# One core, a mixer block with expert lookup: the low half one step later, a pause in the gate build, more rows and loads ahead of stage 2

## The chip, the cores and the metric

One core of one Trainium2 chip runs the whole program. The metric is device time in microseconds: the median of three runs, 3230.48 us before the change.

## What is computed

A block of a language model on 512 tokens of width 2048, in fp32: a mixer (mLSTM and S5 branches), then an expert lookup ("PEER") and a norm. The change lies in the lookup, whose reference is, cut:

```python
s1, i1 = lax.top_k(s[..., 0, :], 16); s2, i2 = lax.top_k(s[..., 1, :], 16)
top_s, pos = lax.top_k(cand_s, 16)            # 8 heads x 16 experts for a token
idx = jnp.take_along_axis(cand_i, pos, axis=-1)
gate = jax.nn.softmax(top_s, axis=-1)
ue = jnp.take(u_tab, it, axis=0)              # u_tab, v_tab: 16384 x 2048
ve = jnp.take(v_tab, it, axis=0)
act = jax.nn.gelu(jnp.einsum('td,ted->te', xt, ue), approximate=False)
out = jnp.einsum('te,ted->td', gt * act, ve)
```

## The kernel before

The lookup is done densely for the experts that many tokens chose, and row by row for the rest. 72 blocks of 128 experts are dense: 28 with fixed numbers (NF) and 44 that the kernel selects (NSEL). Every product of two fp32 tiles is three products of high and low parts (`mm3`, L104 to L106): `split` (L100, L101) makes the high part on ACT and the low part on DVE.

**Stage 1** (1043 to 2191 us) makes gelu(x u) for the 72 blocks, in 72 x 4 steps. `h_step` first calls `u_unit` for the unit two steps ahead: four transposes of the loaded rows ur on PE into a PSUM bank (L1464), uh on ACT, ul on DVE. Then `h_unit` runs 12 matmuls. Every fourth step ends a block: gelu on ACT (L1481), a store to hg_d from SP's queue. `u_load` fetches a block of u_tab by SP, or, for selected blocks, by a gather on POOL's queue.

All orders are written out by hand: each engine runs what the program emits in that order. Beside every step the loop pumps generators against a budget (UBUD). Up to step 117 these are routing, selection and flags (`sides["a"]`). After it (n0) two remain. `gbuild` builds the dense gate table: per 8 tokens five one-hot tiles `go` on DVE, then a `fill`: 24 matmuls (L1419) and two evictions into Gb on ACT (L1420). Each 64 tokens make one Gb (one buffer, 32 KB a partition), stored by four DMAs of 1 MB to gt_d from SP (L1440). GEND sets by which step the table shall be done. `rare` takes the rows outside the dense blocks: 147 for u_tab (w = 0), then 147 for v_tab (w = 1), in token blocks of 54, 36, 31 and 26. Each is a gather of 128 rows, 1 MB, into one of two buffers gr on POOL's queue (L1335), two rows ahead, and a product with accumulation on DVE (L1332 for u, 2.3 us; L1339 for v). A new token block needs its own xa, gathered by the same queue when its first row is due.

**Stage 2** (2222 to 3210 us) multiplies by v_tab in two halves of its columns, 72 units each. `v_load` fetches the activations hgl, gates gt and rows vr of a unit, five units ahead; `v_gate` multiplies hgl by gt (first half only) and stores it to w_d; `v_split` makes ewh, ewl, vh, vl; `v_unit` runs 24 matmuls over all eight PSUM banks. The rows left over are spread evenly over the first 130 units, with two more gr buffers (`rp2`) and gathers four rows ahead. The loads of the first units stand in the program behind the whole of stage 1.

Of the kernel before, what the change touches and what calls it, by code (L numbers as in the profile page):

```python
# [8 lines left out]
F32 = mybir.dt.float32  # L9
# [10 lines left out]
P = 128  # L20
T = 512
# [14 lines left out]
JUNK = F32  # L36
UBUD = 2.5
GEND = 282
VEND = 14
# [7 lines left out]
def hybrid_block(ctx: ExitStack, tc: tile.TileContext, x, norm1_g, w_in, b_gates, conv_w, mnorm_g,  # L47
# [19 lines left out]
    dram = ctx.enter_context(tc.tile_pool(name="dram", bufs=1, space=DRAM))  # L67
    ps = ctx.enter_context(tc.tile_pool(name="ps", bufs=1, space=PSUM))

# [6 lines left out]
    def tp_bank(shape=(P, 512), dtype=F32):  # L76
        return ps.tile(list(shape), dtype, name="tp", bufs=4)

    def mm_bank(shape=(P, 512)):
        return ps.tile(list(shape), F32, name="mm", bufs=4)  # L80

# [1241 lines left out]
    def xa_tile():  # L1323
        UT["m"] = UT.get("m", 0) + 1
        pl = UT["rp2"] if "rp2" in UT and UT["m"] % 2 else UT["rp"]
        return pl.tile([P, D], F32, name="xa")
# [23 lines left out]
    def rare():  # L1350
        q = []
        k = 0
        xa = None
        for n, (w, b, j) in enumerate(rjobs):
            if j == 0:
                xa = xa_tile()
                gather(xa, h1_d if w else xn_d, tokc(b))
            while k < len(rjobs) and k < n + (4 if "rp2" in UT else 2):
                t = gr_tile()
                row_gather(t, rjobs[k][0], rl[:, rjobs[k][1], rjobs[k][2]:rjobs[k][2] + 1])  # L1360
                q.append(t)
                k += 1
            t = q.pop(0)
            a = racts[:, b, j:j + 1]
            if w:
# [41 lines left out]
    def gbuild():  # L1407
# [16 lines left out]
        for c in range(0, T, GC):  # L1424
# [22 lines left out]
    def u_load(i):  # L1447
# [36 lines left out]
    units = [(i, q) for i in range(NT) for q in range(4)]  # L1484
    un = [0]
# [7 lines left out]
    sides["a"] += [route_end(), select(), flags()]  # L1493
    UT["gb_n"] = 0
    UT["rare_n"] = 0
    bud = 0.0
    n0 = None
    for n, (i, q) in enumerate(units):
        h_step(i, q)
        bud += UBUD if n0 is not None else 2.7  # L1500
        while bud > 0:
            if n0 is None and not sides["a"]:
                n0 = n
                sides["a"].append(gbuild())
                sides["g"].append(rare())
            gb_next = n0 is None or UT["gb_n"] * (GEND - n0) <= (n - n0) * (T // 8)
            c = pump1("a") if gb_next else 0
            c = c or (pump1("g") if n0 is not None else 0)
            if not c:
                bud = 0  # L1510
                break
            bud -= c
    drain("a")
    ustk.close()
    xstk.close()

    vp = ctx.enter_context(pool(name="vp", bufs=1))
    UT["rp2"] = vp
    F0 = vp.tile([P, TB, 1024], F32, name="F0")
    vms = ExitStack()  # L1520
    vm = vms.enter_context(pool(name="vm", bufs=1))
    v2h = v2.rearrange("e (h c) -> (e h) c", h=2)
    vunits = [(h, i) for h in range(2) for i in range(NT)]

    def v_load(n):
        h, i = vunits[n]
        vr = vm.tile([P, 1024], F32, name="vr", bufs=6)
        hg = vm.tile([P, T], F32, name="hgl", bufs=6)
        gt = None
        if h:  # L1530
            sp.dma_start(hg, w_d[i])
        else:
            gt = vm.tile([P, T], F32, name="gt", bufs=5)
            sp.dma_start(hg, hg_d[i])
# [10 lines left out]
    def v_gate(n):  # L1545
        vr, hg, gt = UT["l", n]
        if gt is not None:
            v.tensor_tensor(hg, hg, gt, op=OP.mult)  # L1548
            sp.dma_start(w_d[vunits[n][1]], hg)

    def v_split(n):
        vr, hg, gt = UT.pop(("l", n))
# [49 lines left out]
    fin = finish_rare()  # L1602
    for n in range(5):
        v_load(n)
    for n in range(3):
        v_gate(n)
    for n in range(2):
        v_split(n)
    o = banks()
    for n, (h, i) in enumerate(vunits):  # L1610
# [18 lines left out]
        if n >= NV - VEND + 4:  # L1629
            next(fin, None)  # L1630
    vms.close()
    fbs = ExitStack()
    fb = fbs.enter_context(pool(name="fb", bufs=1))
# [49 lines left out]
```

## Time and profile before

| | us |
|---|---|
| median of 3 runs (3226.96 to 3233.34) | 3230.48 |
| the profiled execution | 3238.5 |
| its span, first to last instruction | 3236.7 |
| PE busy | 2930.9 (91%) |
| DVE busy | 2231.2 (69%) |
| ACT busy | 977.8 (30%) |
| POOL busy | 886.5 (27%) |
| mean granted TensorE clock | 0.954 |
| DMA moved 691.9 MB, mean | 214 GB/s |

A row of the profile by line gives: line, engine, operation, out<-in; a time in brackets is how long the engine had been idle and what ended it. PE is busy nearly everywhere by the mean, so what matters is the few stretches where it waits.

### The profile page before, as it was taken

The numbers are of one execution on the slowest core, as the hardware profiler recorded it, in microseconds if no ns is written. First come the engines' busy times: TensorE is split into PE (matmuls) and PEld (weight loads), VectorE is DVE, ScalarE is ACT, GpSimd is POOL, SyncE is SP. The second block draws the span as 40 slices with busy tenths as digits, with TensorE's granted clock in tenths as the row PEclk, the third lists the DMA queues.
The fourth block names the chain that finished last, engine by engine and source line by source line (L and its number), as shares of the span: only waits on it lengthen the run. The fifth ranks groups of instructions, "written<-read, shape, count | busy, mean of one in ns | idle before, by whom it ended". The sixth has DMA issues, their size and how long they took to land. (4 is left out here: it accounts for less than half of the span.)

```text
span 3236.7 us, 44930 instructions
## 1 busy us (share of the span) xinstructions
PE 2930.9 (91%) x17539; PEld 2465.1 (76%) x17540; DVE 2231.2 (69%) x3665; ACT 977.8 (30%) x1491; POOL 886.5 (27%) x656
## 2 busy tenths in 40 slices
PE   7999999999799999998999999985888778898897
PEld 5888978899688888887778887774666666676676
DVE  7468543532488878765667777664878778797885
ACT  5343564432322321122222332221221122222223
POOL 3000111000200000002212222212458788446770
PEclk9999999999899999998999999997999888999998
DMA  4423344343322222624787657669999997999984
GB/s 139 127 85 92 97 114 121 128 149 131 126 92 88 102 84 84 263 109 163 247 263 245 214 155 263 222 221 325 399 366 366 355 392 285 345 382 375 344 323 169
DMA packets 366138, 691.90 MB, mean 214 GB/s; under 512 B 169490, under 2 KB 248850, under 8 KB 320338
## 3 DMA queue, kind: packets, MB, share of 16 engines
q0 software_dynamic: 74240, 393.57, 32.7%
q1 hardware_dynamic: 291680, 295.40, 28.0%
q8 instruction: 139, 2.28, 0.3%
q14 instruction: 79, 0.65, 0.1%
HBM read 644.04 MB, written 96.86 MB: 229 GB/s over the span
## 5 line engine op out<-in xcount | busy, mean ns | idle before, releaser
L104 PE MATMUL mm<-xh,uh 128*128 128x512 f32 x1152 | 484.5, 421 | 0.3 <-ACT uh L100 0.3
L106 PE MATMUL mm<-xh,ul 128*128 128x512 f32 x1152 | 458.0, 398 | 10.8 <-DVE ul L101 10.7
L105 PE MATMUL mm<-xl,uh 128*128 128x512 f32 x1152 | 456.9, 397 | 0.0
L1339 DVE SCALAR_TENSOR_TENSOR xa<-gr,racts,xa 128x2048 f32<-128x2048 f32 x147 | 345.3, 2349 | 112.5 <-DMA gr<-in_peer_v_dram,rl 56.5
L1332 DVE SCALAR_TENSOR_TENSOR junk<-gr,xa 128x2048 f32<-128x2048 f32 x147 | 336.0, 2285 | 98.8 <-DMA gr<-in_peer_u_dram,rl 74.1
L105 PE MATMUL tp<-vl,ewh 128*128 128x512 f32 x576 | 241.8, 420 | 156.3 <-DVE vl L101 156.2
L101 DVE TENSOR_TENSOR wl<-wr,wh 128x1024 fp32r<-128x1024 f32 (+1 forms) x144 | 187.2, 1303 | 241.2 <-ACT wh L100 241.1
L1335 POOL DMA_INDIRECT gr<-in_peer_u_dram,rl x147 | 211.9, 1441 | 358.0 <-DVE junk L1332 288.6
L1335 POOL DMA_INDIRECT gr<-in_peer_v_dram,rl x147 | 254.6, 1732 | 168.7 <-DVE xa L1339 124.8
L100 ACT ACTIVATE ewh<-hgl 128x512 fp32r<-128x512 f32 x144 | 90.9, 631 | 690.0 <-DVE hgl L1548 373.0
L100 ACT ACTIVATE uh<-tp 128x512 fp32r<-128x512 f32 x288 | 171.2, 599 | 422.3 <-PE tp L1464 419.3
L101 DVE TENSOR_TENSOR ul<-tp,uh 128x512 fp32r<-128x512 f32 x288 | 196.7, 686 | 147.2 <-ACT uh L100 147.1
L104 PE MATMUL mm<-wh,xh 128*128 128x256 f32 (+1 forms) x1024 | 294.6, 288 | 0.0
L106 PE MATMUL mm<-wh,xl 128*128 128x256 f32 (+1 forms) x1024 | 288.8, 282 | 1.8 <-DVE xl L101 1.8
L105 PE MATMUL mm<-wl,xh 128*128 128x256 f32 (+1 forms) x1024 | 289.0, 282 | 0.0
L106 PEld LDWEIGHTS mm<-xh,ul 128*128 128x128 f32 x1152 | 220.2, 191 | 65.1 <-DVE ul L101 13.5
L106 PE MATMUL mm<-xh,wl 128*128 128x512 f32 x640 | 256.0, 400 | 12.0 <-DVE wl L101 12.0
L105 PEld LDWEIGHTS tp<-vl,ewh 128*128 128x128 f32 x576 | 114.0, 198 | 199.7 <-DVE vl L101 177.1
L104 PE MATMUL mm<-xh,wh 128*128 128x512 f32 x640 | 258.1, 403 | 0.0
L105 PE MATMUL mm<-xl,wh 128*128 128x512 f32 x640 | 254.9, 398 | 0.0
L104 PE MATMUL tp<-vh,ewh 128*128 128x512 f32 x576 | 232.0, 403 | 24.7 <-ACT vh L100 24.7
L104 PEld LDWEIGHTS mm<-xh,uh 128*128 128x128 f32 x1152 | 221.2, 192 | 38.7 <-ACT uh L100 1.1
(497 smaller groups left out, 6152.5 us busy)
## 6 DMA issues: line engine op xcount, KB each, us to landing
wr<-in_w_in_dram SPq DMA_DIRECT2D x80, 512.0 KB
gt_d<-Gb SPq DMA_DIRECT2D x32, 1024.0 KB
ur<-in_peer_u_dram SPq DMA_DIRECT2D x28, 1024.0 KB
vr<-in_peer_v_dram SPq DMA_DIRECT2D x56, 512.0 KB
hg_d<-hg SPq DMA_DIRECT2D x72, 256.0 KB
hgl<-hg_d SPq DMA_DIRECT2D x72, 256.0 KB
w_d<-hgl SPq DMA_DIRECT2D x72, 256.0 KB
hgl<-w_d SPq DMA_DIRECT2D x72, 256.0 KB
```

Source lines behind the costliest of these rows:

```text
L100: s.activation(hi, src, AF.Copy)
L101: v.tensor_tensor(lo, src, hi.bitcast(F32), op=OP.subtract)
L104: pe.matmul(o, ah, bh, start=start, stop=False)
L105: pe.matmul(o, ah, bl, start=False, stop=False)
L106: pe.matmul(o, al, bh, start=False, stop=stop)
L1332: v.scalar_tensor_tensor(UT["junk"], t, 1.0, xg, op0=OP.mult, op1=OP.mult, accum_out=a)
L1335: g.indirect_dma_start(out=t, out_offset=None, in_=v2 if w else u2, in_offset=IOA(ap=col, axis=0), bounds_check=P * P - 1, oob_is_err=False)
L1339: v.scalar_tensor_tensor(acc, t, a, acc, op0=OP.mult, op1=OP.add)
```

## The change

Six things. (1) `u_unit` makes only the transposes and uh, now three units ahead; the low part is made by `u_low` one step later, two units ahead as before. (2) Stage 1 has its own PSUM pool: three banks tp, two mm, three tu for the transposes; stage 2 opens a third one (4 and 4). (3) After the store of a Gb, `gbuild` isn't pumped for four steps; GEND falls from 282 to 262. (4) The budget per step grows from 2.5 to 2.8 (2.7 to 2.9 before n0), so `rare` gets further under u_tab, the first table. (5) At step 276 (VPRE) the loads of stage 2's first five units are emitted, in a pool of their own. (6) Once rp2 exists, the next token block's xa is gathered six rows ahead, and xa alternates strictly between the two pools.

```diff
-UBUD = 2.5
-GEND = 282
+UBUD = 2.8
+GEND = 262
+VPRE = 276
...
+    def psum_pool(name, tp, mm):
+        if "s" in PS:
+            PS["s"].close()
+        PS["s"] = ExitStack()
+        PS["p"] = PS["s"].enter_context(tc.tile_pool(name=name, bufs=1, space=PSUM, reuse_waits="tile"))
+        PS["tp"], PS["mm"] = tp, mm
...
     def rare():
...
         for n, (w, b, j) in enumerate(rjobs):
+            if n == 0 or nx is None and n + 6 < len(rjobs) and rjobs[n + 6][2] == 0 and "rp2" in UT:
+                nx = xa_tile()
+                gather(nx, h1_d if rjobs[min(n + 6, len(rjobs) - 1)][0] and n else xn_d, tokc(rjobs[n + 6][1] if n else b))
             if j == 0:
-                xa = xa_tile()
-                gather(xa, h1_d if w else xn_d, tokc(b))
+                if nx is None:
+                    nx = xa_tile()
+                    gather(nx, h1_d if w else xn_d, tokc(b))
+                xa, nx = nx, None
...
             for a in range(0, P, 32):
                 sp.dma_start(gv[:, a:a + 32, c:c + GC], Gb[:, a:a + 32, :])
+            UT["hold"] = UT["step"] + 4
...
+    psum_pool("psu", 3, 2)
     u_load(0)
     u_load(1)
...
-        p = tp_bank([P, 4, P])
+        p = PS["p"].tile([P, 4, P], F32, name="tu", bufs=3)
...
-        ul = up.tile([P, 4, P], F32R, name="ul", bufs=4)
-        split(uh, ul, p)
-        UT["u", i, q] = (uh, ul)
+        s.activation(uh, p, AF.Copy)
+        UT["p", i, q] = (uh, p)
...
+    def u_low(i, q):
+        uh, p = UT.pop(("p", i, q))
+        ul = up.tile([P, 4, P], F32R, name="ul", bufs=4)
+        v.tensor_tensor(ul, p, uh.bitcast(F32), op=OP.subtract)
+        UT["u", i, q] = (uh, ul)
...
     def h_step(i, q):
-        while un[0] < len(units) and un[0] < i * 4 + q + 3:
+        n = i * 4 + q
+        while un[0] < len(units) and un[0] < n + 4:
             u_unit(*units[un[0]])
             un[0] += 1
+        while un[1] < len(units) and un[1] < n + 3:
+            u_low(*units[un[1]])
+            un[1] += 1
         h_unit(i, q)
...
     for n, (i, q) in enumerate(units):
         h_step(i, q)
+        if n == VPRE:
+            drain("a")
+            UT["vl"] = vls.enter_context(pool(name="vld", bufs=1, side="right"))
+            for k in range(5):
+                v_load(k)
+        UT["step"] = n
-        bud += UBUD if n0 is not None else 2.7
+        bud += UBUD if n0 is not None else 2.9
...
-            gb_next = n0 is None or UT["gb_n"] * (GEND - n0) <= (n - n0) * (T // 8)
+            gb_next = n0 is None or n >= UT["hold"] and UT["gb_n"] * (GEND - n0) <= (n - n0) * (T // 8)
...
     fin = finish_rare()
-    for n in range(5):
-        v_load(n)
     for n in range(3):
         v_gate(n)
     for n in range(2):
         v_split(n)
+    psum_pool("psv", 4, 4)
```

The order on three engines shows what moves. First DVE, the last steps of stage 1 and the start of stage 2 (junk is the product of one row, go a one-hot tile). Before:

```order
L1431 TENSOR_TENSOR go_21142<-go_21138,DT 128x1024
L101 TENSOR_TENSOR ul<-tp,uh 128x512 x2
L1332 SCALAR_TENSOR_TENSOR junk,racts<-gr,xa 128x2048
L101 TENSOR_TENSOR ul<-tp,uh 128x512
L1332 SCALAR_TENSOR_TENSOR junk,racts<-gr,xa 128x2048
L101 TENSOR_TENSOR ul<-tp,uh 128x512
L1332 SCALAR_TENSOR_TENSOR junk,racts<-gr,xa 128x2048
L101 TENSOR_TENSOR ul<-tp,uh 128x512
L1332 SCALAR_TENSOR_TENSOR junk,racts<-gr,xa 128x2048 x3
L1548 TENSOR_TENSOR hgl<-hgl,gt 128x512 x3
L101 TENSOR_TENSOR ewl<-hgl,ewh 128x512
L101 TENSOR_TENSOR vl<-vr,vh 128x1024
```

Now, the last of 25 steps that hold no go:

```order
L1492 TENSOR_TENSOR ul<-tu,uh 128x512
L1343 SCALAR_TENSOR_TENSOR junk,racts<-gr,xa 128x2048
L1492 TENSOR_TENSOR ul<-tu,uh 128x512
L1343 SCALAR_TENSOR_TENSOR junk,racts<-gr,xa 128x2048 x2
L1492 TENSOR_TENSOR ul<-tu,uh 128x512
L1343 SCALAR_TENSOR_TENSOR junk,racts<-gr,xa 128x2048 x3
L1546 TENSOR_TENSOR hgl<-hgl,gt 128x512 x3
L112 TENSOR_TENSOR ewl<-hgl,ewh 128x512
L112 TENSOR_TENSOR vl<-vr,vh 128x1024
```

Behind step 262 there stood 15 row products among eight groups of go; now there are 29 and no go.

SP's queue, from the last store of the gate table to the loads of stage 2 (gf is the last norm's weight). Before:

```order
L1482 DMA hg_d<-hg 128x512 x5
L1440 DMA gt_d<-Gb 128x32x64 x4
L1482 DMA hg_d<-hg 128x512 x2
L1580 DMA gf<-in_final_g_dram 128x2048
L1534 DMA hgl<-hg_d 128x512
L1537 DMA gt<-gt_d 128x512
L1538 DMA vr<-in_peer_v_dram 128x1024
```

Now:

```order
L1456 DMA gt_d<-Gb 128x32x64 x4
L1505 DMA hg_d<-hg 128x512 x4
L1532 DMA hgl<-hg_d 128x512
L1535 DMA gt<-gt_d 128x512
L1536 DMA vr<-in_peer_v_dram 128x1024
```

and, after the other four units in the same way, up to gf:

```order
L1532 DMA hgl<-hg_d 128x512
L1535 DMA gt<-gt_d 128x512
L1536 DMA vr<-in_peer_v_dram 128x1024
L1505 DMA hg_d<-hg 128x512 x3
L1613 DMA gf<-in_final_g_dram 128x2048
```

The first five units' loads have moved from behind gf to ahead of the last three hg_d stores, and the last gate store stands further from the end.

POOL's queue at the change from the first table to the second (gr is a row's gather, xa the token block's own). Before:

```order
L1335 DMA gr<-in_peer_v_dram,rl 128x2048
L1040 DMA gt<-gt_d,esel 128x512
L1040 DMA vr<-in_peer_v_dram,esel_5726 128x1024
L1335 DMA gr<-in_peer_v_dram,rl 128x2048 x2
L1040 DMA gt<-gt_d,esel 128x512
L1040 DMA vr<-in_peer_v_dram,esel_5726 128x1024
L1040 DMA xa<-h_d,rl 128x2048
L1335 DMA gr<-in_peer_v_dram,rl 128x2048
```

Now:

```order
L1346 DMA gr<-in_peer_u_dram,rl 128x2048 x14
L1051 DMA xa<-xn_d,rl 128x2048
L1346 DMA gr<-in_peer_u_dram,rl 128x2048 x28
L1051 DMA xa<-h_d,rl 128x2048
L1346 DMA gr<-in_peer_u_dram,rl 128x2048 x3
L1346 DMA gr<-in_peer_v_dram,rl 128x2048 x3
L1051 DMA gt<-gt_d,esel 128x512
L1051 DMA vr<-in_peer_v_dram,esel_5726 128x1024
```

The gather of xa from h1_d stood behind gathers of the second table's rows, whose first product needs it; now it stands ahead of the last three gathers of the first table.

## Rows read from the trace of the kernel before

**Rows 1.** Stretches: length; busy PE, PEld, DVE, ACT, POOL (instructions); clock, DMA share, GB/s

```profile
1515.00:2088.00 573.00, 546.68 (x3645) 456.05 (x3644) 415.06 (x563) 164.65 (x292) 136.64 (x106) 0.98 0.71 229
2088.00:2221.00 133.00, 93.41 (x582) 77.34 (x580) 73.33 (x95) 30.21 (x53) 19.77 (x18) 0.87 0.83 260
2221.00:2750.00 529.00, 426.69 (x1677) 339.04 (x1678) 420.82 (x387) 109.95 (x143) 364.07 (x203) 0.90 0.93 358
2750.00:3206.00 456.00, 406.16 (x1735) 330.01 (x1735) 367.37 (x254) 125.47 (x161) 248.91 (x152) 0.95 0.86 335
```

**Rows 2.** PE in order of time: start us, us, instruction; one fill, two steps

```profile
1523.72 1.55 PE L1419 MATMUL tp<-go,go 128*128 128x128 bf16 x24
...
1525.11 0.61 PE L1464 MATMUL tp<-ident,ur 128*128 128x128 f32 x4
...
1528.32 0.60 PE L1464 MATMUL tp<-ident,ur 128*128 128x128 f32 x4
```

**Rows 3.** What PE waited for in stage 1: us, times, longest

```profile
PE tp L1464 <- ACT Gb L1420: 18.5, 3, 8.9
PE tp L1419 <- ACT Gb L1420: 15.2, 2, 9.4
```

**Rows 4.** SP and ACT in order of time: gate stores, and Gb free again

```profile
1669.59 24.63 SPq L1440 DMA_DIRECT2D gt_d<-Gb  x4
...
1699.93 1.09 ACT L1420 ACTIVATE Gb<-tp 128x512 f32<-128x512 f32 x2 [17.11 <-DMA gt_d<-Gb]
...
2088.27 22.55 SPq L1440 DMA_DIRECT2D gt_d<-Gb  x4
```

**Rows 5.** PE and DVE in order of time: from stage 1 to stage 2

```profile
2190.90 0.39 PE L106 MATMUL mm<-xh,ul 128*128 128x512 f32 x1
...
2219.69 0.69 DVE L1548 TENSOR_TENSOR hgl<-hgl,gt 128x512 f32<-128x512 f32 x1 [2.66 <-DMA gt<-gt_d]
...
2220.90 1.22 DVE L101 TENSOR_TENSOR vl<-vr,vh 128x1024 fp32r<-128x1024 f32 x1
...
2222.17 0.79 PE L105 MATMUL tp<-vl,ewh 128*128 128x512 f32 x1 [5.36 <-DVE vl L101]
```

**Rows 6.** POOL and DVE in order of time: two gathers and the product that waited

```profile
2064.90 1.44 POOL L1040 DMA_INDIRECT ur<-in_peer_u_dram,esel  x1 [9.89 <-PE tp L1464]
2066.65 0.99 POOL L1335 DMA_INDIRECT gr<-in_peer_u_dram,rl  x1 [0.30 <-issue]
...
2075.03 2.29 DVE L1332 SCALAR_TENSOR_TENSOR junk<-gr,xa 128x2048 f32<-128x2048 f32 x1 [4.90 <-DMA gr<-in_peer_u_dram,rl]
```

**Rows 7.** DVE in order of time: row products during the last gate store

```profile
2178.12 2.28 DVE L1332 SCALAR_TENSOR_TENSOR junk<-gr,xa 128x2048 f32<-128x2048 f32 x1
...
2181.22 2.28 DVE L1332 SCALAR_TENSOR_TENSOR junk<-gr,xa 128x2048 f32<-128x2048 f32 x1
...
2188.23 2.29 DVE L1332 SCALAR_TENSOR_TENSOR junk<-gr,xa 128x2048 f32<-128x2048 f32 x1 [3.81 <-DMA gr<-in_peer_u_dram,rl]
...
2199.18 2.29 DVE L1332 SCALAR_TENSOR_TENSOR junk<-gr,xa 128x2048 f32<-128x2048 f32 x1 [2.64 <-DMA gr<-in_peer_u_dram,rl]
```

**Rows 8.** What DVE waited for in stage 2: us, times, longest

```profile
DVE xa L1339 <- DMA xa<-h_d,rl: 52.8, 4, 14.4
...
DVE junk L1332 <- DMA xa<-xn_d,rl: 16.5, 2, 8.8
```

**Rows 9.** ACT in order of time: start of unit 72, and two units late

```profile
2750.60 0.61 ACT L100 ACTIVATE ewh<-hgl 128x512 fp32r<-128x512 f32 x1
...
3139.89 0.64 ACT L100 ACTIVATE ewh<-hgl 128x512 fp32r<-128x512 f32 x1 [3.85 <-PE mm L105]
...
3145.33 0.63 ACT L100 ACTIVATE ewh<-hgl 128x512 fp32r<-128x512 f32 x1 [3.86 <-PE mm L105]
```

**Rows 10.** Stretches of stage 2, columns as in rows 1

```profile
2407.00:2520.00 113.00, 96.96 (x378) 76.92 (x377) 91.79 (x96) 23.83 (x31) 94.70 (x55) 0.91 0.92 347
...
2800.00:2920.00 120.00, 116.28 (x505) 93.81 (x503) 107.35 (x72) 33.34 (x43) 53.65 (x36) 1.00 0.97 388
```

More of the change, by code (lines that the diff above doesn't have):

```diff
@@ L67, in hybrid_block @@
     dram = ctx.enter_context(tc.tile_pool(name="dram", bufs=1, space=DRAM))
-    ps = ctx.enter_context(tc.tile_pool(name="ps", bufs=1, space=PSUM))
+    PS = {}
+    def psum_pool(name, tp, mm):
[4 more added lines that the diff above has]
+        PS["tp"], PS["mm"] = tp, mm
+    psum_pool("ps", 4, 4)
+    ctx.callback(lambda: PS["s"].close())
     u_d = dram.tile([8, 8, 128, 64], F32, name="u_d")
@@ L76, in tp_bank @@
     def tp_bank(shape=(P, 512), dtype=F32):
-        return ps.tile(list(shape), dtype, name="tp", bufs=4)
+        return PS["p"].tile(list(shape), dtype, name="tp", bufs=PS["tp"])
     def mm_bank(shape=(P, 512)):
-        return ps.tile(list(shape), F32, name="mm", bufs=4)
+        return PS["p"].tile(list(shape), F32, name="mm", bufs=PS["mm"])
     ident = consts.tile([P, P], F32, name="ident")
@@ L1323, in xa_tile @@
     def xa_tile():
-        UT["m"] = UT.get("m", 0) + 1
-        pl = UT["rp2"] if "rp2" in UT and UT["m"] % 2 else UT["rp"]
+        pl = UT["rp2"] if "rp2" in UT and UT.get("xp") is UT["rp"] else UT["rp"]
+        UT["xp"] = pl
         return pl.tile([P, D], F32, name="xa")
@@ L1352, in rare @@
         k = 0
-        xa = None
+        xa = nx = None
         for n, (w, b, j) in enumerate(rjobs):
+            if n == 0 or nx is None and n + 6 < len(rjobs) and rjobs[n + 6][2] == 0 and "rp2" in UT:
+                nx = xa_tile()
+                gather(nx, h1_d if rjobs[min(n + 6, len(rjobs) - 1)][0] and n else xn_d, tokc(rjobs[n + 6][1] if n else b))
             if j == 0:
-                xa = xa_tile()
-                gather(xa, h1_d if w else xn_d, tokc(b))
+                if nx is None:
+                    nx = xa_tile()
+                    gather(nx, h1_d if w else xn_d, tokc(b))
+                xa, nx = nx, None
             while k < len(rjobs) and k < n + (4 if "rp2" in UT else 2):
@@ L1484, in hybrid_block @@
     units = [(i, q) for i in range(NT) for q in range(4)]
-    un = [0]
+    un = [0, 0]
     def h_step(i, q):
-        while un[0] < len(units) and un[0] < i * 4 + q + 3:
+        n = i * 4 + q
+        while un[0] < len(units) and un[0] < n + 4:
             u_unit(*units[un[0]])
             un[0] += 1
+        while un[1] < len(units) and un[1] < n + 3:
+            u_low(*units[un[1]])
+            un[1] += 1
         h_unit(i, q)
[L1493 to L1499, printed above, removed]
-        bud += UBUD if n0 is not None else 2.7
[L1501 to L1505, printed above, removed]
-            gb_next = n0 is None or UT["gb_n"] * (GEND - n0) <= (n - n0) * (T // 8)
[L1507 to L1521, printed above, removed]
     v2h = v2.rearrange("e (h c) -> (e h) c", h=2)
@@ L1526, in v_load @@
         h, i = vunits[n]
-        vr = vm.tile([P, 1024], F32, name="vr", bufs=6)
-        hg = vm.tile([P, T], F32, name="hgl", bufs=6)
+        vr = UT["vl"].tile([P, 1024], F32, name="vr", bufs=6)
+        hg = UT["vl"].tile([P, T], F32, name="hgl", bufs=6)
         gt = None
@@ L1532, in v_load @@
         else:
-            gt = vm.tile([P, T], F32, name="gt", bufs=5)
+            gt = UT["vl"].tile([P, T], F32, name="gt", bufs=5)
             sp.dma_start(hg, hg_d[i])
@@ L1549, in v_gate @@
             sp.dma_start(w_d[vunits[n][1]], hg)
+    sides["a"] += [route_end(), select(), flags()]
+    vls = ExitStack()
+    UT["gb_n"] = UT["hold"] = 0
+    UT["rare_n"] = 0
+    bud = 0.0
+    n0 = None
+    for n, (i, q) in enumerate(units):
+        h_step(i, q)
+        if n == VPRE:
[5 more added lines that the diff above has]
+        bud += UBUD if n0 is not None else 2.9
+        while bud > 0:
+            if n0 is None and not sides["a"]:
+                n0 = n
+                sides["a"].append(gbuild())
+                sides["g"].append(rare())
+            gb_next = n0 is None or n >= UT["hold"] and UT["gb_n"] * (GEND - n0) <= (n - n0) * (T // 8)
+            c = pump1("a") if gb_next else 0
+            c = c or (pump1("g") if n0 is not None else 0)
+            if not c:
+                bud = 0
+                break
+            bud -= c
+    ustk.close()
+    xstk.close()
+    vp = ctx.enter_context(pool(name="vp", bufs=1))
+    UT["rp2"] = vp
+    F0 = vp.tile([P, TB, 1024], F32, name="F0")
+    vms = ExitStack()
+    vm = vms.enter_context(pool(name="vm", bufs=1))
     def v_split(n):
@@ L1631, in hybrid_block @@
     vms.close()
+    vls.close()
     fbs = ExitStack()
```

## The prediction

> **What bounds the kernel now.** I read the stretches first [rows 1]. From 1515 to 2088 us, the part of stage 1 that builds the gate table, PE is busy 547 of 573 us: PE sets the pace there. From 2221 on, in stage 2, PE is busy 427 of 529 us and the DMA engines 0.93 of the time; in the second half PE has 406 of 456 and the DMA 0.86. So stage 2 is paced by what feeds PE: bytes in its first half, single waits in its second. Between them, 2088 to 2221, PE loses 40 of 133 us.
>
> A step of stage 1 (one q) takes PE 3.21 us, and a gate fill adds 1.39 [rows 2]. PE waits there mostly for the eviction of a gate fill, 18.5 + 15.2 = 33.7 us [rows 3], because ACT sits in front of the one buffer Gb until its store has landed: issued at 1669.6, Gb free at 1699.9 [rows 4]. At the end PE finishes stage 1 at 2191.3 and runs freely again from 2222.2, 31 us later: the last store and then the first loads of stage 2 stand in the way [rows 5].
>
> The profiled execution took 3238.5 us, 8.0 over the median 3230.48. The sum is made against 3238.5, and 8.0 is taken off at the end. A difference under about 0.2% (6.5 us) can't be told from no change.
>
> **The parts.** The order shows what moves. Rows of the first table done before stage 2: 115 instead of 85. Of them 29 instead of 15 stand behind step 262, where all fills are now over.
>
> *Low part a step later, own PSUM ring.* The same instructions. DVE's ul no longer asks for the transposes of its own step, so it runs up to one step further ahead of PE. PE is the bound there, so 0 by itself. The rings shrink (tp 4 to 3, mm 4 to 2): fills alone use tp in that section, and mm has four steps per bank. Should the cover go, that is, should DVE be late by a step, the price is 3.21 a time.
>
> *Pause after a store.* Counted in PE's order, the first fill after stores 1 to 7 stands 6, 5, 5, 5, 5, 5, 5 steps behind the store; now 5, 5, 6, 5, 5, 5, 5. The first one-hots of the next block are made in the same call that issues the store, and after the pause the builder catches up at once. So the distance ACT needs is not there, and I take 0 of the 33.7 us.
>
> *Fills end at step 262.* By that step PE has done 64 fills, not 56: 8 x 1.39 = **+11 us** until there. DVE was busy 415 of 573 us in this section [rows 1]; 16 more rows at 2.3 and eight more groups of one-hots at their budget of 3.45 make 480, still under PE.
>
> *Tail, step 262 to the first free matmul of stage 2.* Before: the seventh store at 2088.3 [rows 4] to 2222.2 [rows 5], 134 us. Now 25 steps of 3.21 are 80 us for PE, but DVE has 29 row products, each on its own 1 MB gather into one of two buffers, and the ul of later steps stand behind them on DVE. A gather is issued when the product on its buffer ends. One gather alone has no row; two issued 1.75 us apart (ur, then gr) land 10.1 us after the first, 8.4 after the second [rows 6]. One alone takes between 5.1 (half) and 8.4; I take 5.6, near the half, since transfers of one queue mostly follow each other. With the product 2.29 and 0.35 to the next issue a buffer turns in 8.2 us, a row per 4.1; the four ur gathers still to come make it 4.35. 29 x 4.35 = 126. Under the last store rows came 21.1 us for four gaps, 5.3 each [rows 7], five of them: +8 with the extra burst on the queue. Row 90 now falls there with its fresh xa: about 8, as the two such waits of 16.5 us [rows 8]. The five early loads are 5 x 1.3 MB on the same engines, 18 us at 358 GB/s, half of it in gaps: +8. The handover itself is three hgl of 0.69, ewl and vl of 1.22 on DVE [rows 5], 4 us, as the operands lie ready: the 31 us are gone, but the rows have taken their place. Sum 154, **+20 us**. Ends: PE's own 80 us and 4, as if no row were waited for, -50; 5.3 for each row, 182, +48.
>
> The Trainium skill, "DMA: Bandwidth & Descriptors", section "Anatomy of one DMA", gives a fixed 2.0 us plus bytes over 436 GB/s; for 1.05 MB that is an estimate of 4.4 us, a row per 3.5 and a tail about 25 us shorter than mine, 3116 in all. No row here shows a lone gather, and the pair [rows 6] is slower than two of these in a row (8.8 against 10.1).
>
> *SP.* The early loads stand before the last three hg_d stores. They need the last gate store landed, 14 steps (45 us) earlier, against 30 us for a store [rows 4]. So 0; if they had to wait, hg, then uh, would stop behind them.
>
> *Stage 2, first half.* 179 rows instead of 209 over 130 units: 1.38 a unit, not 1.61. Bytes were 358 GB/s x 529 us = 189 MB [rows 1]. Less 17 rows x 1.05 and five units already loaded, 6.6: 165 MB. At 358 GB/s that is 460 against 528 (2222.2 to 2750.6 [rows 5, 9]): **-68 us**. The rate could be the 388 of a stretch without a wait on xa, or the 348 of one with row-wise loads [rows 10]: 425 or 491, so -103 to -37. PE needs 72 x 5.44 = 392 [rows 9], so bytes still bind.
>
> *Stage 2, second half.* DVE waited 52.8 us in four places for xa from h1_d, up to 14.4, and 16.5 for xn_d [rows 8]; now xa is gathered six rows ahead once rp2 exists. Three of the four lie behind 2750 us, some 39 us. Also 17 products at 2.3, 39 us more, leave DVE, which was busy 367 of 456 [rows 1]. With both, PE paces: 72 x 5.44 + 11 for the change of half and the finish = 403 against 456: **-53 us**. Ends: -25 (only part of each wait reaches PE) and -60.
>
> Sum: 3238.5 + 11 + 20 - 68 - 53 = 3148.5; less 8.0, **3141 us**.
>
> **The rivals.**
> 1. *The tail runs at PE's pace.* A lone gather lands fast, rows come each 3.1 us as the first gap under the store [rows 7]: 29 x 3.1 + 8 + 8 + 4 = 110, so -24 instead of +20: 3097. For it: only 1.3 MB a step are asked. Against: two buffers and the pair of [rows 6]. The rule above points this way.
> 2. *Fewer rows help stage 2 little*, since the row-wise loads keep 348 GB/s [rows 10] and waits return at other rows: -37 and -35 in place of -68 and -53: 3190.
> 3. *The pause works after all*, because the lag leaves PE more uh to run on; then the 33.7 us [rows 3] go: 3107. Against: the distance of five steps, and three tp banks stop the second fill.
> 4. *Slower: the tail drowns.* Rows, ur, the last store and the early loads share the engines; one gap there was 7.0 us [rows 7]. At 8 a row the tail is 29 x 8 + 28 = 260, +126. With rival 2's stage 2 at the same time (the gathers queue up) this gives 3238.5 + 11 + 126 - 37 - 35 - 8 = 3296; with my stage 2, 3247. It turns slower from about 7.4 us a row on.
>
> **How the numbers follow.** Forecast 0.60, its own range 3105 to 3175 by the ends of the tail and the rate. Rival 1: 0.12, rival 2: 0.14, rival 3: 0.06, rival 4: 0.08. The range 3090 to 3200 holds the forecast, rivals 1 to 3 nearly whole, and leaves rival 4 and the extremes out. Faster by over 0.2%: 0.60 + 0.12 + 0.06 and 0.10 of rival 2 = 0.88; its last 0.04 within; slower 0.08.
>
> **What would show it.** PE still waiting some 30 us on Gb evictions, with store to Gb free at 30 us. Behind step 262, DVE waiting on gr at nearly every row, rows 4 to 5 us apart, PE waiting for ul. A handover of under 10 us after the last row product, hgl without a DMA wait. Stage 2's first half in 450 to 475 us with DMA above 0.9; the second in about 405 with no xa wait over 3 us and the clock near 1.0. Wrong would be: Gb waits gone, rows at 3.2 us in the tail, xa waits still there, or a first half above 500 us.

## The result, and the profile after

The changed kernel takes 3187.71 us, median of 4 runs (3182.46 to 3194.73), beside 3228.72 us (3223.79 to 3233.34) for the kernel before on the same chip: ratio 0.9875, interval 0.9849 to 0.99. It is faster, by 41 us where I had forecast 89. The profiled execution took 3185.52 us (span 3183.6), and my sum for it was 3148.5: 37 us are missing.

The same four stretches as [rows 1] show where, with the columns of that group. For the changed kernel they are: from its first row gather to its last gate store (step 262), the tail from there to the free run of stage 2, and the two halves of stage 2.

```profile
1480.00:2144.00 664.00, 602.58 (x3995) 502.01 (x3994) 480.60 (x645) 180.67 (x321) 157.04 (x129) 0.95 0.72 237
2144.00:2292.00 148.00, 93.78 (x384) 72.45 (x383) 81.59 (x86) 19.66 (x35) 38.81 (x35) 0.81 0.88 308
2292.00:2754.00 462.00, 405.14 (x1680) 321.14 (x1679) 384.97 (x339) 112.69 (x143) 320.15 (x187) 0.97 0.95 366
2754.00:3153.00 399.00, 395.28 (x1731) 326.60 (x1731) 335.77 (x240) 124.36 (x161) 223.93 (x134) 0.99 0.89 356
```

Tail, first half and second half are what the sum had: 148 for 154, 462 for 460, 399 for 403. The whole miss lies in the first stretch: the store of step 262 was issued at 2088.27 before [rows 4], I had forecast 2099, and it came at 2143.62. It is 55 us late where I had +11. (The first stretch of [rows 1] begins 12 us behind the first row gather. From that gather to this store the kernel before takes 585 us, from 1502.82, and the change 660, from 1483.25.)

What was waited for in that stretch (us in total, times, longest), first before, from 1502 to 2088, where the 18.5 us of [rows 3] belong too:

```profile
DVE junk L1332 <- DMA gr<-in_peer_u_dram,rl: 32.4, 12, 10.0
...
PE mm L106 <- DVE ul L101: 10.7, 2, 9.1
...
PE tp L1419 <- ACT Gb L1420: 5.8, 1, 5.8
```

And in the change, from 1480 to 2144:

```profile
ACT Gb L1436 <- DMA gt_d<-Gb: 100.0, 7, 27.0
...
DVE junk L1343 <- DMA gr<-in_peer_u_dram,rl: 87.4, 17, 11.6
...
PE tu L1482 <- DVE ul L1492: 35.5, 13, 10.2
PE tp L1435 <- ACT Gb L1436: 25.9, 4, 9.9
```

DVE waits 87 us for rows, 55 more than before. The ul stand behind them on DVE, and PE waits for ul to free its transposes' ring: 35.5 us, for 10.7 before. PE's wait for Gb, which the store gives back, is still there beside it but has hardly grown: 25.9 us, for 24.3 (18.5 and 5.8).

The handover, DVE and ACT in order of time, against [rows 5]: the last row product, three hgl without a wait for a DMA, and ewh of the first unit.

```profile
2285.70 2.29 DVE L1343 SCALAR_TENSOR_TENSOR junk<-gr,xa 128x2048 f32<-128x2048 f32 x1 [1.32 <-DMA gr<-in_peer_u_dram,rl]
...
2287.92 1.92 DVE L1546 TENSOR_TENSOR hgl<-hgl,gt 128x512 f32<-128x512 f32 x3
...
2288.64 0.63 ACT L111 ACTIVATE ewh<-hgl 128x512 fp32r<-128x512 f32 x1 [7.76 <-DVE hgl L1546]
```

Of stage 2's waits on DVE, the 52.8 us for xa from h1_d [rows 8] are gone; what its accumulation of xa still waits for are rows, as long as before (56.5 us):

```profile
DVE xa L1350 <- DMA gr<-in_peer_v_dram,rl: 56.8, 52, 5.4
```

### The profile page after: what moved, and what is told of

The parts are those of the page before. It is cut to its first block, busy times and chain, and to the rows that moved or that the text cites. A ratio compares the mean times of both kernels' runs of the same rounds, so it can differ in the third digit from the quotient of the medians.

```text
span 3183.6 us, 44978 instructions
## 1 busy us (share of the span) xinstructions
PE 2926.7 (92%) x17540; PEld 2462.5 (77%) x17540; DVE 2226.3 (70%) x3665; ACT 978.8 (31%) x1491; POOL 848.9 (27%) x656
## 5 line engine op out<-in xcount | busy, mean ns | idle before, releaser
L115 PE MATMUL mm<-xh,uh 128*128 128x512 f32 x1152 | 494.6, 429 | 0.0
L117 PE MATMUL mm<-xh,ul 128*128 128x512 f32 x1152 | 465.1, 404 | 7.5 <-DVE ul L1492 7.5
L116 PE MATMUL mm<-xl,uh 128*128 128x512 f32 x1152 | 465.3, 404 | 0.0
L1484 ACT ACTIVATE uh<-tu 128x512 fp32r<-128x512 f32 x288 | 171.6, 600 | 501.4 <-PE tu L1482 489.4
L1346 POOL DMA_INDIRECT gr<-in_peer_u_dram,rl x147 | 180.2, 1226 | 460.8 <-DVE junk L1343 419.1
L116 PE MATMUL tp<-vl,ewh 128*128 128x512 f32 x576 | 232.5, 404 | 61.1 <-DVE vl L112 61.0
L116 PEld LDWEIGHTS mm<-xl,uh 128*128 128x128 f32 x1152 | 227.5, 197 | 39.6
L1482 PE MATMUL tu<-ident,ur 128*128 128x128 f32 x1152 | 182.1, 282 | 73.0 <-DVE ul L1492 72.3
L111 ACT ACTIVATE wh<-wr 128x1024 fp32r<-128x1024 f32 (+1 forms) x144 | 166.8, 1161 | 260.5 <-PE mm L117 103.0
```

What stands on the lines that cost most here:

```text
L111: s.activation(hi, src, AF.Copy)
L115: pe.matmul(o, ah, bh, start=start, stop=False)
L116: pe.matmul(o, ah, bl, start=False, stop=False)
L117: pe.matmul(o, al, bh, start=False, stop=stop)
L1346: g.indirect_dma_start(out=t, out_offset=None, in_=v2 if w else u2, in_offset=IOA(ap=col, axis=0), bounds_check=P * P - 1, oob_is_err=False)
L1484: s.activation(uh, p, AF.Copy)
```

## The experiments

Each was timed beside the kernel before on the same chip; ratios are to that. Times inside a kernel come from its own profiled execution.

**The parts one by one.** First the change without its pause.

```
-            UT["hold"] = UT["step"] + 4
```

> The changed kernel without the pause after a store. The first gather to the last gate store took 664 us in the changed kernel, some 44 more than I had added up. Theory P: the pause drops rows back to back under the store, where DVE waits for them; without it this section falls to 630-645 and the whole to about 3160-3170. Theory R (the rows themselves, 86 instead of 70, are too many for what brings them): the order shows the pause to move only a handful of rows by a step, so the section stays at 655-670 and the whole within 8 us of 3188; PE's wait for Gb stays where it is (about 26 us).

Measured: 3193.67 us, 0.9891 (0.9864 to 0.9918), first gather to last store 669 us. The intervals overlap with the change's own: the pause is worth nothing that can be told. Theory P falls. In the profiled executions PE's waits did change, and against each other: without the pause PE waits 46.8 us for Gb (25.9 with it) and 22.9 for ul (35.5).

Next, the old budget of side work, that is, fewer rows.

```
-UBUD = 2.8
+UBUD = 2.5
...
-        bud += UBUD if n0 is not None else 2.9
+        bud += UBUD if n0 is not None else 2.7
```

> The changed kernel with the old budget of side work (2.5 a step, 2.7 before the builder starts): fewer rows before stage 2, 82 against 111 up to the last gate store's end by the order, nothing else changed. Theory R (rows wait, DVE is late with ul, PE stops): the last gate store is issued near 2105 us instead of 2143.6, DVE's wait for gr before it falls from 87 us towards 35; the tail shortens from 148 to about 115 (16 rows behind the store instead of 29); stage 2 takes the rows back: first half about 490 instead of 462, second about 410 instead of 399. Whole: 3150-3170, so faster than the change itself. Theory P or any that blames the lag or the early loads: the section is as lossy as now (last store near 2130-2140) and with the longer stage 2 the whole is 3195-3215.

Measured: 3224.81 us, 0.9986 (0.9973 to 0.9999). The last store came at 2112 (2105 expected) and DVE's wait for gr fell to 57 us, so the rows do make the stretch slow: 602 us with 61 rows, 660 with 87. But the tail still took 131 us with 24 rows, and the two halves of stage 2 paid 515 and 433 us, for 462 and 399. The 30 rows cost 31 us up to the last store and 17 in the tail, and save 53 and 34 in stage 2: more than half of what they save is paid back. They are worth 37 us in all by the medians, some 1.2 us a row.

The other parts, each put alone into the kernel before: the early xa gather, the low part a step later with its PSUM rings, and the early end of the fills with the early loads. Their edits are the change's own hunks of those names, so only the heads are shown.

```
+            if n == 0 or nx is None and n + 6 < len(rjobs) and rjobs[n + 6][2] == 0 and "rp2" in UT:
+                nx = xa_tile()
...
```

> The kernel before with nothing but the xa gather six rows ahead and its buffers taken in turn. Theory X (each wait for xa passes on to PE): DVE's waits for xa (52.8 us in four places) go, the second half of stage 2 falls from 455 to 415-425, the first stays within 10 of 529: whole 3185-3200. Rival (the second half fell because 17 row products left it, the xa waits were covered by the operands in hand): second half 445-455, whole 3215-3230.

Measured: 3202.19 us, 0.9914 (0.9882 to 0.9945). Stretches of stage 2, to be held against the last two of [rows 1]:

```profile
2228.00:2744.00 516.00, 422.16 (x1678) 336.17 (x1679) 422.86 (x389) 111.38 (x143) 370.61 (x205) 0.90 0.95 368
2744.00:3173.00 429.00, 405.35 (x1731) 330.66 (x1731) 365.53 (x253) 125.17 (x160) 248.01 (x150) 0.98 0.91 355
```

The second half fell from 456 to 429, a little less than theory X had it (415-425) and its rival had 445-455: xa's waits did reach PE. The first half fell by 13 as well, where X allowed 10.

```
+    psum_pool("psu", 3, 2)
...
+        while un[1] < len(units) and un[1] < n + 3:
+            u_low(*units[un[1]])
```

> The kernel before with nothing but the low part a step later and the PSUM rings (tp 3, mm 2, tu 3 in stage 1). Theory Z (0 by itself, as I predicted): 3222-3236. Theory T (three tp banks instead of four cost the routing work before the gate section something: the run with the old budget reached step 112 at 1501 us against 1494): step 112 near 1500, whole 3233-3245. Theory H (a step more of slack lets DVE's waits for rows pass PE by): PE's waits for ul and Gb in the gate section fall, whole 3205-3220.

Measured: 3220.66 us, 0.9964 (0.9948 to 0.998): 12 us faster. It lies at the edge of theories Z and H; PE's wait for Gb in the gate section fell from 24.3 to 10.7 us, that for ul rose from 10.7 to 17.4. So H, weakly.

```
-GEND = 282
+GEND = 262
+VPRE = 276
...
+        if n == VPRE:
+            drain("a")
...
```

> The kernel before with nothing but the fills ending at step 262 and the five loads of stage 2 at step 276. Theory of my prediction: the 31 us from the last product of stage 1 to the free run of stage 2 go, and the rows behind step 262 (about 24 by the run with the old budget) take some of it: last store near 2100, first matmul of stage 2 near 2210, whole 3205-3215. Theory N (the run with the old budget was only 5 us faster than before although its xa part alone is worth 28, so something in it loses some 20): the rows that bunch behind the last store cost over 5 us each and the first half of stage 2 does not shorten, whole 3230-3250.

Measured: 3267.04 us, 1.0103 (1.0071 to 1.0136). This part of the change, alone, makes the kernel 35 us **slower**. ACT's gelu of step 263 (the 66th hg) is a mark that lies at the same step in every kernel; before, and with the early end alone:

```profile
2090.85 0.60 ACT L1481 ACTIVATE hg<-mm 128x512 f32<-128x512 f32 x1 [2.12 <-PE mm L106]
```

```profile
2130.45 0.60 ACT L1482 ACTIVATE hg<-mm 128x512 f32<-128x512 f32 x1 [1.99 <-PE mm L107]
```

It is 40 us later, of which eight fills are 11. About half of the rest stands among PE's waits for Gb in this run, from its first gather to its last store; the granted clock of the same stretch (columns as in [rows 1]) is lower too, 0.95 against 0.98 before:

```profile
PE tp L1420 <- ACT Gb L1421: 21.9, 4, 6.4
PE tp L1465 <- ACT Gb L1421: 17.7, 3, 10.5
```

```profile
1498.00:2128.00 630.00, 573.74 (x3850) 480.06 (x3849) 419.37 (x582) 173.56 (x310) 119.93 (x100) 0.95 0.65 205
```

The builder has one more block to fill in the same steps, so PE comes back to the one Gb once more and with fewer steps between: 39.6 us of waiting for it, against 24.3.

Together: -28 (xa), -12 (low part), +35 (early end and loads), -37 (rows), about 0 (pause) give -42; the change as a whole gave -41. The parts add up: the run with the old budget holds all of them but the rows, and was 5 us faster than before, as -28, -12 and +35 give.

**The same part undone in the change.** Fills to step 282 and loads behind stage 1 again, rows and all else as changed; and only the loads put back.

```
-GEND = 262
-VPRE = 276
+GEND = 282
...
+    drain("a")
     ustk.close()
...
+    UT["vl"] = vls.enter_context(pool(name="vld", bufs=1, side="right"))
+    for n in range(5):
+        v_load(n)
```

> The changed kernel with the fills ending at step 282 again and the five loads of stage 2 behind stage 1, as in the kernel before; rows (113 by the order), lag, pause and xa as in the change. Theory F (the early end of the fills is what the change loses by: done alone it made the kernel before 35 us slower, since eight more returns to the one Gb come on steps that are packed closer): step 263 falls from 2146 to about 2110, the handover at the last store costs its 30 us again, stage 2 starts near 2255 instead of 2292, whole 3148-3160. Rival (the early end pays once there are 30 more rows, which fill its tail while PE goes on): stage 2 starts no earlier than 2285, whole 3180-3200.

Measured: 3155.18 us, 0.9774 (0.975 to 0.9797). This is theory F by the time; the "eight more returns" of the expectation are eight more fills and one more return to Gb. The mark of step 263, in the change and here:

```profile
2146.20 0.60 ACT L1504 ACTIVATE hg<-mm 128x512 f32<-128x512 f32 x1 [2.12 <-PE mm L117]
```

```profile
2122.37 0.60 ACT L1503 ACTIVATE hg<-mm 128x512 f32<-128x512 f32 x1 [2.13 <-PE mm L116]
```

So of the 55 us until there, 24 are the early end (11 of them the fills themselves), and 31 are there with the late end too, with the rows. The run with the old budget divides them in the same way from the other side: it has the early end and not the rows, and passes the mark at 2115.00, 24 us behind the kernel before and 31 ahead of the change.

> The changed kernel with its fills ending at step 262 as in the change, but the five loads of stage 2 behind stage 1 again: the early loads alone undone. Theory E (the early loads are what the early end is for; they hide a wait of 25-30 us for them at the start of stage 2, and the early end's own price is higher than the 33 us of both together): whole 3200-3215, with hgl waiting 15-30 us for its loads. Rival (the rows fill that time anyway, the loads only take engines from them): 3180-3195, and the tail shorter by what the loads took, 5-10 us.

Measured: 3194.95 us, 0.9898 (0.9867 to 0.9929), at the upper end of the rival's range, but the tail did not get shorter (151 us). The interval overlaps with the change's, so the early loads are worth between nothing and some 10 us. This run and the one before it differ in nothing but the step by which the fills end, 262 or 282: 40 us. It is the early end that costs, not the loads.

**Buffers, lag, pause.** A third gr buffer in stage 1, gathers three rows ahead.

```
-        t = pl.tile([P, D], F32, name="gr", bufs=2)
+        t = pl.tile([P, D], F32, name="gr", bufs=3 if pl is UT["rp"] else 2)
...
-            while k < len(rjobs) and k < n + (4 if "rp2" in UT else 2):
+            while k < len(rjobs) and k < n + (4 if "rp2" in UT else 3):
```

> The changed kernel with three gr buffers in stage 1 instead of two, gathers issued three rows ahead. Theory R2 (the round trip of a gather on two buffers sets the row's pace): DVE's wait for gr in the gate section falls from 87 us below 35 and in the tail from 58 below 25; last store near 2110, tail 110-120 instead of 148, stage 2 as now: 3110-3130 in all. Rival B (bytes: the DMA engines are 0.88 busy in the tail and the store takes them in the section): the gathers only queue longer, waits fall by a third at most, tail about 140, last store 2130-2140: 3165-3185.

Measured: 3163.31 us, 0.9802 (0.9783 to 0.9822). R2 was right on the tail, 123 us, and wrong on the section, which kept its 661, so its 3110-3130 were missed too; rival B was nearly right on the whole. Waits from first gather to last store, then the section and the tail as stretches:

```profile
ACT Gb L1436 <- DMA gt_d<-Gb: 122.4, 7, 26.5
...
PE tp L1435 <- ACT Gb L1436: 51.7, 6, 13.4
DVE junk L1343 <- DMA gr<-in_peer_u_dram,rl: 30.2, 5, 10.7
PE tu L1482 <- DVE ul L1492: 16.9, 5, 13.2
```

```profile
1480.00:2144.00 664.00, 595.40 (x3977) 498.10 (x3976) 482.03 (x647) 178.64 (x319) 168.62 (x130) 0.95 0.73 238
2144.00:2268.00 124.00, 89.78 (x389) 70.32 (x387) 80.30 (x85) 20.56 (x36) 43.07 (x35) 0.86 1.00 366
```

DVE's wait for rows fell from 87.4 to 30.2 us and PE's for ul from 35.5 to 16.9, and PE's wait for Gb, held by the store, took their place, 51.7 for 25.9. One wait hid the other. In the tail the DMA engines are now busy all the time.

Four variants of it: the low part back in its own step (the old rings of four), the pause at 8 steps, the late end (with the pause at 4), and a middle way (fills to step 272, loads at 284, the pause at 8).

```
-        s.activation(uh, p, AF.Copy)
-        UT["p", i, q] = (uh, p)
+        ul = up.tile([P, 4, P], F32R, name="ul", bufs=4)
+        split(uh, ul, p)
```

> The changed kernel with three gr buffers (3163 us) and the low part back in its own step, with the old PSUM rings of four and four. Theory Z or T (the lag is worth nothing, or its smaller rings cost up to 8 us): 3150-3165, and step 112 earlier by 0 to 8 us. Theory H (the lag is what lets rows be waited for without PE stopping): PE's waits for ul in the gate section rise from 17 us to 35 or more, whole 3175-3190.

Measured: 3163.53 us, 0.9794 (0.9767 to 0.9821). Beside more rows and three buffers the low part a step later is worth nothing, and its rings cost nothing.

```
-            UT["hold"] = UT["step"] + 4
+            UT["hold"] = UT["step"] + 8
```

> The changed kernel with three gr buffers (3163 us) and the pause after a store 8 steps instead of 4: by the order the first fill then stands 8 steps behind the store instead of 6 or 7, and eight rows lie between. Theory G (with the row waits gone the loss of the gate section is the eviction that waits for the store: 51.7 of its 66 us of PE waits): those fall under 20 us, the section from 661 to 620-635, whole 3120-3140. Rival S (rows under the store lengthen its landing from 30 us by as much as the pause gives, and the one-hots then come in a burst that DVE can't follow): PE's waits for Gb stay at 30 or more or turn into waits for ul, section 650-670, whole 3150-3175.

Measured: 3154.32 us, 0.9756 (0.9728 to 0.9785), section 653. Rival S: waits for Gb fell to 22.5 us, those for ul doubled to 34.4, and DVE's for rows rose to 73.2. The pause puts rows where Gb was waited for, and ul pays.

> The same with three gr buffers. Three buffers gave 25 us with the early end, all of it in the tail behind the last store (148 to 123), none in the gate section. Theory F and tail: with the late end there is no such tail, so they give little here, 0 to 10 less than the run without them: 3140-3155. Rival (rows waited for anywhere hold PE up): another 20-25 less, 3125-3135.

Measured: 3156.88 us, 0.9774 (0.975 to 0.9798), as without the third buffer: it helps only a tail.

> The changed kernel with three gr buffers, a pause of 8 steps (3154 us together), the fills ending at step 272 and the early loads at step 284: half way between the two ends. If each step of closer packing costs and the tail's rows are what the early end leaves uncovered, this lies between: step 263 near 2125, the tail's six rows near PE's own pace, stage 2 starting near 2245, whole 3130-3145. If the early loads by themselves are what costs (their 6.6 MB on the engines that bring the rows), nothing is won: 3150-3165.

Measured: 3152.66 us, 0.9762 (0.9739 to 0.9785), stage 2 running freely from 2252. Nothing was won, though not for the reason given, since the loads alone cost nothing. Six versions now stand between 3152 and 3164, whichever wait they shorten.

**What a row costs there.** Two kernels that leave something out: the first all row gathers of stage 1, the second nearly all of each row product.

```
-                t = gr_tile()
-                row_gather(t, ...)
+                t = None
+                if "rp2" in UT:
+                    t = gr_tile()
+                    row_gather(t, ...)
...
+            t = xa if t is None else t
```

> The changed kernel without the row gathers of stage 1: each of those row products still runs, at full length, but on xa alone, so the 115 gathers of 1 MB are left out and nothing is waited for. Theory B (a row's price in the gate section is its bytes: they lie in the store's way and DVE waits for them in front of ul): from the first row to the last gate store 610-625 us instead of 661, PE's waits for Gb under 10 us, behind the store 90-105 us instead of 148, whole 3080-3110. Theory D (the price is the 2.3 us of DVE itself, in order ahead of ul and the one-hots): section 645-660, behind the store 115 or more, whole 3140-3165.

```
+        c = D if "rp2" in UT else 16
+        v.scalar_tensor_tensor(UT["junk"][:, 0:c], t[:, 0:c], 1.0, xg[:, 0:c], ...)
```

> The changed kernel with the gathers as they are, but each row product of stage 1 on 16 columns instead of 2048 (the rest of the sum is left out), so DVE spends a small part of its 2.3 us on each. Theory B: the section falls by under 15 us, since DVE still waits for every row in order, and the tail stays above 125 us; whole 3160-3185. Theory D: section 610-630, tail 100-115, whole 3095-3120.

Measured: 3059.56 us, 0.9468 (0.9443 to 0.9493) without the gathers; 3164.41 us, 0.9795 (0.9765 to 0.9825) without the products. Section and tail without gathers, then without products:

```profile
1480.00:2072.00 592.00, 581.68 (x3984) 488.14 (x3983) 481.98 (x646) 180.08 (x320) 59.44 (x40) 0.99 0.47 139
2072.00:2159.00 87.00, 79.30 (x383) 64.19 (x383) 78.30 (x85) 19.74 (x34) 9.33 (x6) 0.99 0.65 209
```

```profile
1480.00:2143.00 663.00, 599.43 (x3990) 501.05 (x3989) 299.57 (x647) 179.93 (x321) 134.04 (x129) 0.95 0.72 238
2143.00:2275.00 132.00, 89.87 (x383) 69.54 (x382) 22.68 (x83) 19.70 (x35) 33.73 (x34) 0.86 0.96 345
```

This is theory B, and clear of its rival. With DVE at its full 482 us but no bytes, the section takes 592 us instead of 664 and the tail runs at PE's own pace; with 181 us less of DVE's work but all bytes, the section is as long as ever. Without the gathers PE waits 2.4 us for Gb and 7.9 for ul, and passes the mark of step 263 at 2074, earlier than the kernel before with its 2090.85: PE is idle for only 10 us of this section, so the early end, too, can cost little beyond its fills where no rows are brought. An obvious rival is that the gathers of ur, for selected blocks, stand behind the rows on POOL's queue; but in this section of the change the profile shows PE waiting for ul and Gb, never for ur.

Where the bytes hurt was looked for in the 30 us behind one gate store (first line of each pair), and between that and the next store (second line). The kernel before, the change, and the change without row gathers; DMA share and GB/s stand last (a share can pass 1, since a packet's whole time is counted where it starts):

```profile
1670.00:1700.00 30.00, 22.73 (x130) 18.55 (x128) 16.27 (x22) 3.01 (x7) 4.12 (x4) 0.96 1.08 307
1705.00:1757.00 52.00, 52.00 (x378) 43.68 (x377) 39.58 (x56) 16.24 (x29) 11.07 (x10) 1.00 0.65 231
```

```profile
1735.00:1765.00 30.00, 24.53 (x132) 20.01 (x130) 19.68 (x26) 6.21 (x12) 7.54 (x6) 0.94 1.05 302
1770.00:1814.00 44.00, 44.00 (x326) 37.17 (x324) 36.66 (x50) 14.90 (x26) 10.98 (x10) 1.00 0.36 125
```

```profile
1706.00:1736.00 30.00, 30.00 (x186) 25.00 (x185) 25.70 (x34) 8.77 (x16) 2.34 (x2) 1.00 0.87 229
1740.00:1778.00 38.00, 38.00 (x276) 32.01 (x276) 32.01 (x44) 11.65 (x21) 4.62 (x3) 1.00 0.27 97
```

PE loses 7 and 5 of the 30 us behind these two stores, and nothing between them and the next. Behind a store the engines are full or nearly so: 0.90 to 1.11 with rows, 0.83 to 0.98 with the store and ur alone. The mean of 0.72 is made of these and of stretches well below it.

These are single stores, and over the seven that another one follows the picture is a different one. In the 30 us behind them PE stands still 26 us in all before, 25 in the change, 28 without products and 2 without gathers; on the rest of the way to the next store, 11, 24, 25 and 0. So the bytes make both losses, but what the change added is not behind the stores. It is between them, and what PE waits longer for in this section are the ul behind rows.

Gb was free 28.3 us after the store of 1735.09, and 19.6 us after that of 1706.47, by the next eviction on ACT, in the change and without gathers. The seven stores give 22.2 to 40.7 us, mean 30.6, and 19.5 to 24.9, mean 22.0; before, 20.4 to 33.4, mean 27.5.

```profile
1763.34 1.08 ACT L1436 ACTIVATE Gb<-tp 128x512 f32<-128x512 f32 x2 [5.67 <-DMA gt_d<-Gb]
```

```profile
1726.02 1.09 ACT L1439 ACTIVATE Gb<-tp 128x512 f32<-128x512 f32 x2 [3.06 <-DMA gt_d<-Gb]
```

**The version this points to.** Rows are held back for 7 steps behind each store, what is not spent is kept for the steps after (up to 3.0), and a budget of 3.2 brings the same number of rows. Both versions have three gr buffers, one with the fills ending at step 272, one with the late end; the runs to hold them against are the middle way (3152.66, whose pause of 8 steps is back at 4 here) and the late end with three buffers (3156.88).

```
+            UT["quiet"] = UT["step"] + 7
...
-            c = c or (pump1("g") if n0 is not None else 0)
+            c = c or (pump1("g") if n0 is not None and n >= UT["quiet"] else 0)
             if not c:
-                bud = 0
+                bud = min(bud, 3.0)
```

> Rows held back for 7 steps after each gate store instead of the fills for 8, and the budget of 3.2 a step brings the same number of rows on the steps between; else as the run with the fills ending at step 272, early loads at 284 and three gr buffers (3153 us). Theory W (the 30 us behind a store are where the DMA engines are over 1.0 busy, behind them 0.36 to 0.69, so a row costs only there): from the store to Gb free 20-22 us instead of 28, PE's waits for Gb under 10 us and for ul under 15, last store near 2145 instead of 2169, whole 3115-3130. Rival Q (rows packed on fewer steps wait for each other and DVE is late with ul between the stores): waits for ul rise to 50 or more, last store as now or later, whole 3150-3170.

> The same holding back of rows in the run with the late end of the fills and late loads (three gr buffers, 3157 us). Theory W: step 263 at 2100-2108 instead of 2123, whole 3130-3145. Rival Q: 3150-3170.

Measured: 3125.76 us, 0.9675 (0.9647 to 0.9702), and 3130.66 us, 0.9696 (0.966 to 0.9732). Each is 26 to 27 us faster than the run to hold it against, with the same number of rows before stage 2, and the first is 2% under the change. Its profiled execution took 3137.5 us, 12 above its median. Its waits from 1480 to 2147, and the eviction behind its store of 1738.94:

```profile
PE tu L1483 <- DVE ul L1493: 38.9, 14, 11.6
DVE junk L1343 <- DMA gr<-in_peer_u_dram,rl: 21.4, 9, 8.3
...
PE tp L1435 <- ACT Gb L1436: 9.3, 3, 7.0
```

```profile
1758.82 1.09 ACT L1436 ACTIVATE Gb<-tp 128x512 f32<-128x512 f32 x2 [0.67 <-DMA gt_d<-Gb]
```

Gb is free 19.9 us after this store; the seven give 19.9 to 30.2, mean 25.2, so they lie between the change and the run without gathers. The times are theory W's, its mechanism is borne out in part only. PE's waits for Gb are mostly gone, but those for ul stayed where they were (38.9 us; 39.3 in the middle way), and with the late end one took the other's place. PE's waits up to step 263, with the late end and three buffers and then with the rows held back as well:

```profile
PE tp L1434 <- ACT Gb L1435: 44.2, 5, 12.0
PE tu L1481 <- DVE ul L1491: 13.2, 8, 11.4
```

```profile
PE tu L1482 <- DVE ul L1492: 46.0, 12, 13.5
PE tp L1434 <- ACT Gb L1435: 6.3, 3, 4.4
```

Packed rows make DVE late between the stores, as rival Q said. So the mark of step 263 is passed only 3 us earlier in both versions (2128.61 for 2131.64, and 2120.10 for 2123.11, where W had 2100 to 2108), and the first one's last store came at 2165, not 2145. Most of the gain in the profiled executions lies behind the last store, from which PE needs 71 and 35 us to the free run of stage 2, for 83 and 51. That fits rows that are no longer in the way of that store and of the loads behind it, but it was not tried by itself.

## Why the prediction was right in direction and too large

- **The rows until step 262: the step that failed.** I wrote "DVE was busy 415 of 573 us", worked out 480, "still under PE", and so charged the 16 more rows in the gate section nothing; the bytes I did not charge at all, with the DMA engines at 0.71 in [rows 1]. DVE's 480.60 came out to the digit, and it was beside the point. A row's price there is its 1 MB, which other rows, and the ul behind them on DVE, wait for, and which stands in the way of the gate store: 31 us until step 263, by the late end and by the old budget alike. PE's waits for ul grew from 10.7 to 35.5 us, those for Gb only from 24.3 to 25.9; without the gathers they are 7.9 and 2.4.
- **Fills end at step 262, +11.** The eight fills are 11, but PE also returns to Gb once more and sooner, and the granted clock was lower (0.95 for 0.98 with this part alone): 24 in the change, 40 alone. This term was mis-sized by 13 and is the second half of the miss.
- **The handover, 31 us gone.** It went, to 4 us, as forecast. But the rows that the early end leaves bunched behind the last store took its place and more, so the early end with the early loads lost 35 us alone. My +20 for the tail had its size right (148 for 154); I had not set that +20, which already holds the -31, beside the +11 and asked whether the early end should gain at all.
- **Why the tail is slow.** I named the two-buffer turn. A third buffer took 25 of the 64 us over PE's own 84, and the DMA engines were then full (1.00 at 366 GB/s); without the rows' bytes the tail takes 87. The lower end I had given (-50) is that case.
- **The row's pace in the tail.** The rule that I set against [rows 6], the Trainium skill's "DMA: Bandwidth & Descriptors", section "Anatomy of one DMA", gives an estimate of 3.5 us a row. Even without products the tail's 27 rows took 132 us, 4.9 each with the ur and the handover among them; the trace does not bear it out here.
- **Pause 0**: right as a sum, but not for the reason given, that the distance to the store stays the same. It took 21 us off PE's waits for Gb and put 13 on those for ul. **Low part 0**: 12 us better alone, nothing beside three buffers.
- **Stage 2, -68 and -53**: right, 462 and 399, for the reasons given: bytes in the first half (0.95 at 366 GB/s), PE in the second (395 of 399, clock 0.99). xa alone brought 27 of the second half, where I had put 39. Two slips of mine did not enter the sum. At 348 GB/s the 165 MB take 474 us and not 491, so the lower end of the first half was -54 and not -37. And 17 of the 30 rows leave the first half, so 13 products leave DVE in the second, 30 us, and not 17.
- **The rivals.** Rival 2's 3190 (3173 with the slip put right) is nearest to the result, but its cause did not happen: stage 2 gained all I forecast. That the result lies inside 3090 to 3200 is luck in the same way. No rival had a gate section that becomes slower.

## What to carry to other kernels

Before calling moved transfers free, read the DMA share stretch by stretch, above all right behind a transfer that something waits for, and not as a mean over the section: 0.72 here was 1.05 in the 30 us behind the stores and 0.55 between them. Then sum the waits over all such stretches, not in one of them: PE lost as much between the stores (24 us) as behind them (25). To price an operation that brings data and works on it, leave out the bytes in one run and the work in another; the two answers here were 128 and 23 us. When one of two waits on the same engines is shortened and the time stays, look whether the other has grown: here Gb and ul changed places in four runs. With the late end a third buffer brought nothing, and holding the rows back behind each store 26 us.

## What was not expected of the hardware

Where PE stalled, more was lost than the stalls themselves. The section holds the same work with and without the row gathers (3995 and 3984 matmuls), and PE is busy 602.58 us at a mean granted clock of 0.95 in the one and 581.68 at 0.99 in the other: of the 72 us between them 21 are in PE's busy time, on top of 51 us of idle time. The clock has two levels, 2.4 and 1.2 GHz; the stretch with the lower mean is the one in which PE had stood still for ul and Gb. By the clock's records the lower level holds for 61 us of it, and for 10 us without the gathers. That the lower clock is the whole of those 21 us was not tried by itself.
